# A two-block fp32 kernel whose queue orders are planned from TensorE's due times

## The chip, the core and the metric

The kernel runs on one core of a Trainium2 chip. A core has TensorE (PE: matmuls, with weight loads written PEld), VectorE (DVE), ScalarE (ACT), GpSimd (POOL) and SyncE (SP, which here only issues DMAs); POOL issues some DMAs too. Each engine works through its own queue strictly in order: an instruction that waits for another engine or for a DMA holds up everything behind it on its engine. PE's clock is granted by a throttle, and the profile tells the granted share. The metric is the device time of one execution in microseconds (us), and the median of several runs is compared.

## The reference, cut to what matters

Two transformer-like blocks follow each other on 512 tokens of width 2048, all in fp32. The first block puts 16 meta tokens ahead (528 rows) and has two mixers, A (grouped attention with axial rotary positions, 8 query heads, 2 key/value heads) and B (difference of two softmaxes, 8 heads). The second has stick-breaking attention (8 heads) and a gated linear recurrence (LRU, 8 blocks of channels).

```python
# first block
hn = rmsnorm(h, pre_norm_g)
qa, ka, va, ga, qb, kb, vb, gb = split(hn @ w_in)
ya = gqa_axial_mixer(qa, ka, va, ...) * silu(ga)       # softmax(q k^T) v per head
yb = diff_attn_mixer(qb, kb, vb, ...) * silu(gb)       # (softmax(s1) - lam*softmax(s2)) v, rmsnorm per head
h = h + rmsnorm(concat([ya, yb]) @ w_out, post_norm_g)
# second block
q, k, v, g_sb, x_lru, g_lru = split(rmsnorm_2(h) @ w_in_2)
y_sb  = stick_breaking_attention(rmsnorm_2(q), rmsnorm_2(k), v) * silu(g_sb)
y_lru = rg_lru(causal_depthwise_conv(x_lru)) * silu(g_lru)
out = h[meta removed] + concat([y_sb, y_lru]) @ w_out_2
```

## The kernel before

**Exact products from halves.** Every fp32 operand of a matmul is split into a high and a low half of type fp32r. The helper `split` (lines 167 to 169) casts on ACT (L168) and subtracts on DVE (L169). Each product is then three passes on PE (`PASSES`, line 396): high x high, high x low, low x high. So each tile of weights costs a DMA, an ACT cast and a DVE subtraction before PE can use it: `wraw` holds weights as loaded, `wsp` the halves. All matmuls are issued in `mm` (L201) and all transposes in `tr` (L204), so the tile names tell them apart in a profile: `pj` is a projection, `pss` scores or a transposed block, `ptt` the transposed probabilities, `pmt` the product of probabilities and values, `bank` the scores of the second block.

**Stages.** Keys, values and queries of A are projected first (to about 176 us of the span). Then follow 20 pairs of 128-column weight blocks (8 pairs for the two gates, 12 for q, k and v of B), each done by `seven` (line 431): a two-by-two scheme with seven products instead of eight on 12 of the 16 K tiles, the rest (`rest`) in the plain way. Its weight operands are sums of raw weight blocks, which accumulating DMAs form: `sum_up` (L356) issues them on POOL's queue, `load_raw` (L352) the plain loads on SP's, and `produce` (line 358) splits each operand and starts the next load into the slot that comes free. `side_x` (line 631) prepares the sums of activations for it (tiles `x23`, `x1s`). While `seven` runs for the gates (176 to about 370 us) attention of A goes on beside it, and after that attention of B. Then come the first output projection (O1), the second block's projections (XL, GL, GS, v, qk; weights through `load_next`, L320), its recurrence and attention beside these, and the second output projection (O2).

**A head of B.** `b_scores` (line 887) copies the new q and k into operand tiles, and then makes eight score tiles of 128 x 528: four matmuls into the only `pss` buffer, a DVE instruction that adds the bias and finds the minimum (L921), an ACT exponential (L924), and per pair two reciprocals, an ACT scaling (L936) and a DVE combination (L937). `b_sums` (line 943) calls `pv_steps` (line 696), which transposes the probabilities (`ptt`), splits them (`pt`, and `ptail`, L717 to L719, for the last 16 keys), multiplies with the values, normalises each head (L967 to L975) and sends it to DRAM (`yd`, L976). `fetch_y` (L618) reads it back and splits it into `big`, from which O1 reads. The projection of the next head may overwrite q and k when `b_scores` has copied them (key `qkused`).

**Who sets the order on PE.** Each piece of work is a Python generator. `run` (line 228) keeps a clock, to which each matmul adds an estimate of its time, and calls the first generator whose keys are all due: sides first, `main_work` last. A step that has handed work to another engine writes into `ready`, through `post(key, ns)` (line 210), when PE may go on with what depends on it: the clock plus `ns` times `pace[0]` plus 300 ns. From the first gate pair to the last value pair of B `pace[0]` is 1.35, else 1. Successive matmuls are tied by order-only edges (`_queue`, line 192), so PE's order is just the order in which the generators issued.

**Who sets the order elsewhere.** For ACT, DVE, POOL and SP there are no such edges, but for a few `issue_after` blocks that put activations behind a table load or another activation. Their queues come from the tile framework's own scheduler, which fills them by its own cost estimates.

Of the kernel before, what the change touches and what calls it, by code (L numbers as in the profile page):

```python
# [2 lines left out]

# [104 lines left out]
    return [(("KA", i), h) for h in range(2) for i in range(2)] + [(u, h) for u in seq for h in range(2)]  # L108


@with_exitstack
def hybrid_two_block_kernel(ctx: ExitStack, tc: tile.TileContext, wp, wq, wc, xT, xtok, par, lvec, cst, rg, pg, lruw, out):
    nc = tc.nc
    ctx.enter_context(nc.allow_low_precision("float32r halves of exact float32 splits"))
    act, dve, pool = nc.scalar, nc.vector, nc.gpsimd

    sb = ctx.enter_context(tc.tile_pool(name="sb", bufs=1))
    psj = ctx.enter_context(tc.tile_pool(name="psj", bufs=4, space=bass.MemoryType.PSUM))
# [1 line left out]
    dram = ctx.enter_context(tc.tile_pool(name="dram", bufs=1, space=bass.MemoryType.DRAM))  # L120

    def T(shape, tag, dt=F32, bufs=1):
        return sb.tile(shape, dt, tag=tag, name=tag, bufs=bufs)

    def small(n):
        return T([P, 16], "sm", F32, 16)[:, :n]

    def pjt():
        return psj.tile([P, 512], F32, tag="pj", name="pj")

    def evac2(dst, ps):

# [4 lines left out]
    pss_pool = [pss_stack.enter_context(tc.tile_pool(name="pss", bufs=1, space=bass.MemoryType.PSUM))]  # L137

    def pst():
        return pss_pool[0].tile([P, 2, 512], F32, tag="pss", name="pss")  # L140

    def pst_banks():

        return pss_pool[0].tile([P, 512], F32, tag="bank", name="bank", bufs=2)

    def ptt():
        return ps1.tile([P, 4, P], F32, tag="ptt", name="ptt")

    def pmt():
        return ps1.tile([P, 512], F32, tag="pmt", name="pmt")  # L150

    def et(n=L):
        return T([P, L], "e", F32, 6)[:, :n]
# [51 lines left out]

    HOP = 300.0

    pace = [1.0]

    def post(key, ns=0.0):  # L210
        ready[key] = state["clock"] + (ns * pace[0] + HOP if ns else 0.0)

    def hold(key):
        ready[key] = math.inf
# [10 lines left out]
    def when(*keys):  # L225
        return keys
# [27 lines left out]
    class Later:  # L254


        def __init__(self, make):
            self.make, self.tile = make, None
# [6 lines left out]
        def __getitem__(self, index):  # L265
            return self.whole()[index]

    turn = [None]

    def next_turn(shapes):  # L270

        if turn[0]:
            turn[0].close()
        turn[0] = ExitStack()
        pool_ = turn[0].enter_context(tc.tile_pool(name="turn", bufs=1))
        return [pool_.tile(sh, dt, tag=f"turn{i}", name=name) for i, (name, sh, dt) in enumerate(shapes)]

    early = Later(lambda: next_turn([("early", [P, KT * NTOK], F32)])[0])
    XO = 2 * KS * L
# [349 lines left out]
    gins = [0]  # L629

    def side_x():
        yield when(("kr", 0), ("kr", 1))

        def fetch(j):
            x = et(), et()
            for t, kt in zip(x, (j, KS + j)):
                nc.sync.dma_start(t, xT[kt])
# [138 lines left out]
    def side_kv(g):  # L776
        if g == 0:
            kt_[0] = T([P, 2, 2, L], "kk", F32R)
        yield when(("kv", 1), "rnat", "pss")
        kb, t1, u = (early[:, (3 * g + i) * 640 : (3 * g + i + 1) * 640] for i in range(3))  # L780
        dve.memset(kb[:, 512:640], 0.0)
        tp = flat(pst())
        for j in range(5):
            n = P if j < 4 else NM
            tr(tp[:n, j * P : (j + 1) * P], kvraw[g][:, tile_cols(j)], ident)
        dve.tensor_tensor(blocks(kb)[:, :4], blocks(tp[:, :512]),
                          rnat[:, 0:4].unsqueeze(2).broadcast_to([P, 4, P]), ALU.mult)
# [99 lines left out]
    def b_scores(h, e):  # L887
# [23 lines left out]
        def scores(qt, m, l):  # L911
# [4 lines left out]
            for c in range(2):  # L916
# [3 lines left out]
            b0 = 384 - qt * P  # L920
            dve.tensor_tensor_reduce(out=halves(x), in0=s[:, :, :HL], in1=halves(bias[:, b0 : b0 + L]),  # L921
                                     scale=1.0, scalar=3e38, op0=ALU.add, op1=ALU.min, accum_out=nm)
# [20 lines left out]
    def b_sums(h, e, vt):  # L943
# [19 lines left out]
        ssp = pmt()  # L963
        mm(ssp, ones_r, sh, True, False)
        mm(ssp, ones_r, sl, False, True)
        with tc.issue_after(lnload[0]):
# [75 lines left out]
    def side_lru(b):  # L1042
# [31 lines left out]
            pss_stack.close()  # L1074
            pss_pool[0] = ctx.enter_context(tc.tile_pool(name="psb", bufs=2, space=bass.MemoryType.PSUM))
        if b % 4 == 3:
            with tc.issue_after(ins):
# [15 lines left out]
    def sb_scores(h, e, vt):  # L1093
# [24 lines left out]
        for hf in range(2):  # L1118
            yield when(("qkt", h), "pss", "calm", 2)
            take_e(2)  # L1120
            for q2 in range(2):
# [3 lines left out]
                for pi, (a, b) in enumerate(PASSES):  # L1125
# [5 lines left out]
                with tc.issue_after(lnload[1]):  # L1131
# [43 lines left out]
    def main_work():  # L1175
# [88 lines left out]
        with tc.issue_after(last_tanh[0]):  # L1264
            lnload[0] = act.preload_act_table_set("natural_log_exp_and_others").ins

        ysplit = set()
# [135 lines left out]
        for h in range(8):  # L1403
# [4 lines left out]
        with tc.issue_after(ins):  # L1408
            lnload[1] = act.preload_act_table_set("natural_log_exp_and_others").ins

        def sb_v(c):
# [10 lines left out]
        def sb_qk(c):  # L1422
# [21 lines left out]
            yield from tm([("qk", c, kg) for kg in kgs], 0, evac, kgs, range(NT), *extra)  # L1444
            for t in range(NT):
                sq = et(512)
                with tc.issue_after(last[0]):
# [156 lines left out]
```

## Time and profile before

| | |
|---|---|
| median of 3 runs | 1773.55 us (1773.48 to 1774.43) |
| the profiled execution's own time | 1770.61 us |
| its span, first to last instruction | 1768.8 us |
| busy: PE / DVE / ACT / POOL | 1700.2 / 1110.1 / 902.2 / 151.6 us |
| matmuls, weight loads | 10288 each |
| mean granted clock of PE | 0.986 |

Durations and waits come from the profiled execution. A line of a view by stretches has the busy time of each engine within a stretch of the span and the granted clock there. A line of the order of time has start, duration, engine, line and operation, the tiles written and read, and in square brackets the engine's idle time before it and who ended that. "A <- B: t, n, m" says that A waited t us for B in n waits, m the longest. An "L" number is a line of the kernel, and a line of a helper stands for all that call it.

### The profile page before, as it was taken

To read this page: it belongs to the slowest core of one execution; us is meant where nothing else is said; L and a number is where in the kernel's file an instruction comes from. 1 tells how busy PE (TensorE), PEld (TensorE's weight loads), DVE (VectorE), ACT (ScalarE), POOL (GpSimd) and SP (SyncE) were. 2 spreads that over 40 slices of the span, in tenths; PEclk is the share of its full clock that TensorE was granted. 3 is DMA by queue.
4 is the path that set the end of the run, shared out by engine and by line. 5 is a ranking of instruction groups with operands and counts; after the bars stand their busy time and mean duration, and the time that the engine had idled before them with its cause. 6 is when DMAs were issued, how large, how long until landed. Compare 5 with 4: busy or idle time off the path is not lost.

```text
span 1768.8 us, 26488 instructions
## 1 busy us (share of the span) xinstructions
PE 1700.2 (96%) x10288; PEld 1509.4 (85%) x10288; DVE 1110.1 (63%) x1861; ACT 902.2 (51%) x1493; POOL 151.6 (9%) x165
## 2 busy tenths in 40 slices
PE   8999989998999898899699999999999999999999
PEld 7789889998999888888588999888888888888887
DVE  5774687776688777786358767843323575486433
ACT  6454555566466656566345547742222564475311
POOL 0111121211121121101000000100000000000000
PEclk9999999999999899999899999999999999999999
DMA  8436766765566454553267764233322222432223
GB/s 299 158 128 142 189 143 166 168 170 128 126 151 146 104 138 99 135 185 90 72 214 262 227 187 149 92 96 96 96 94 90 83 79 73 142 120 84 84 85 130
DMA packets 85550, 239.58 MB, mean 135 GB/s; under 512 B 9632, under 2 KB 15392, under 8 KB 83744
## 3 DMA queue, kind: packets, MB, share of 16 engines
q1 hardware_dynamic: 73904, 206.43, 36.6%
q0 software_dynamic: 11520, 31.46, 11.2%
q8 instruction: 80, 1.31, 0.3%
q14 instruction: 46, 0.38, 0.1%
HBM read 220.03 MB, written 17.83 MB: 134 GB/s over the span
## 4 chain that ended last, share of the span: by engine, by line
PE 56%; DVE 1%; DMA 1%; ACT 0%; issue 0%; DVEq 0%; ACTq 0%; SPq 0%
PE pj L201 51%; PE pmt L201 2%; PE pss L201 1%; PE bank L201 1%; PE ptt L204 1%; PE pmt L204 0%; PE pss L204 0%; DMA wraw<-in_wp 0%; DMA wraw<-in_wq 0%; DVE wsp L169 0%; DMA yd<-xmisc 0%; DMA e<-yd 0%; DVE pt L169 0%; ACT wsp L168 0%; DVE ptail L719 0%
## 5 line engine op out<-in xcount | busy, mean ns | idle before, releaser
L201 PE MATMUL pj<-wsp,big 128*128 128x512 f32 x3072 | 738.0, 397 | 10.2 <-ACT big L168 10.2
L201 PEld LDWEIGHTS pj<-wsp,big 128*128 128x128 f32 x3072 | 571.8, 189 | 138.4 <-ACT big L168 10.6
L201 PE MATMUL pj<-big,wsp 128*128 128x264 f32 (+3 forms) x4320 | 636.4, 304 | 15.1 <-ACT big L546 5.5
L169 DVE TENSOR_TENSOR wsp<-wraw,wsp 128x1024 fp32r<-128x1024 f32 (+3 forms) x399 | 426.1, 1070 | 336.8 <-ACT wsp L168 329.7
L201 PEld LDWEIGHTS pj<-big,wsp 128*128 128x128 f32 x4320 | 581.3, 189 | 53.2 <-ACT xmisc L457 5.9
L168 ACT CAST wsp<-wraw 128x1024 fp32r<-128x1024 f32 (+3 forms) x399 | 366.9, 922 | 459.3 <-PE pj L201 349.4
L356 POOL DMA_DIRECT2D wraw<-in_wq x80 | 70.0, 888 | 467.1 <-DVE wsp L169 294.3
L201 PE MATMUL pj<-x,wsp 128*128 128x264 f32 x720 | 98.7, 288 | 0.5 <-DVE wsp L169 0.5
L201 PEld LDWEIGHTS pj<-x,wsp 128*128 128x128 f32 x720 | 93.2, 192 | 0.8 <-DVE wsp L169 0.7
L201 PE MATMUL pmt<-pt,vv 128*128 128x256 f32 (+1 forms) x528 | 75.9, 296 | 16.8 <-DVE ptail L719 14.1
L201 PEld LDWEIGHTS pmt<-pt,vv 128*128 128x128 f32 x528 | 72.4, 203 | 21.0 <-DVE ptail L719 14.7
L201 PE MATMUL pss<-kk,qq 128*128 128x264 f32 x448 | 76.4, 300 | 7.4 <-DVE sm L921 7.1
L169 DVE TENSOR_TENSOR pt<-ptt,pt 128x512 fp32r<-128x512 f32 (+2 forms) x96 | 59.3, 618 | 27.1 <-ACT pt L168 26.7
L201 PEld LDWEIGHTS pss<-kk,qq 128*128 128x128 f32 x448 | 65.2, 198 | 11.9 <-DVE sm L921 7.6
L924 ACT ACTIVATE e<-e,sm 128x528 f32<-128x528 f32 x64 | 47.1, 736 | 38.5 <-DVE sm L921 38.0
L168 ACT CAST pt<-ptt 128x512 fp32r<-128x512 f32 (+2 forms) x96 | 50.3, 524 | 28.5 <-PE ptt L204 28.0
L204 PE MATMUL ptt<-ident,e 128*128 128x128 f32 x336 | 53.9, 278 | 8.6 <-DVE e L937 6.2
L921 DVE CUSTOM_DVE_ANT_0 e<-pss,ar 128x528 f32<-128x528 f32 x64 | 44.9, 702 | 26.0 <-PE pss L201 25.6
L1129 POOL TENSOR_SCALAR_AFFINE_SELECT e<-e 128x128 f32<-128x128 f32 x32 | 12.8, 401 | 478.7 <-ACT e L1128 470.8
L204 PEld LDWEIGHTS ptt<-ident,e 128*128 128x128 f32 x336 | 40.6, 142 | 12.8 <-DVE e L937 6.7
L201 PE MATMUL pj<-x1s,wsp 128*128 128x264 f32 x360 | 48.6, 285 | 2.4 <-DVE e L1241 2.4
L201 PEld LDWEIGHTS pj<-x1s,wsp 128*128 128x128 f32 x360 | 45.8, 188 | 2.9 <-DVE e L1241 2.6
(254 smaller groups left out, 1391.3 us busy)
## 6 DMA issues: line engine op xcount, KB each, us to landing
wraw<-in_wp SPq DMA_DIRECT2D x215, 512.0 KB, 3.6
wraw<-in_wq SPq DMA_DIRECT2D x80, 384.0 KB, 4.0
wraw<-in_wq POOLq DMA_DIRECT2D x80, 384.0 KB, 5.0
wraw<-in_wc SPq DMA_DIRECT2D x40, 256.0 KB, 3.2
e<-in_xT SPq DMA_DIRECT2D x28, 264.0 KB, 3.8
early<-in_xtok SPq DMA_DIRECT2D x4, 1024.0 KB, 6.9
gated<-e SPq DMA_DIRECT2D x16, 256.0 KB, 3.6
e<-yd SPq DMA_DIRECT2D x16, 256.0 KB, 3.7
```

Of the source, the lines that this page charges most:

```text
L168: act.copy(hi, src)
L169: dve.tensor_tensor(lo, src, f(hi), ALU.subtract)
L201: _queue(nc.tensor.matmul(out, lhsT, rhs, start=start, stop=stop).ins, cost)
L204: _queue(nc.tensor.transpose(out, in_, identity).ins, 110.0)
L356: pool.dma_start(pair_raw[(p, r)], wq[p, q], accum_op=ALU.add)
L921: dve.tensor_tensor_reduce(out=halves(x), in0=s[:, :, :HL], in1=halves(bias[:, b0 : b0 + L]), scale=1.0, scalar=3e38, op0=ALU.add, op1=ALU ...
L924: act.activation(x, x, AF.Exp, scale=-1.0, bias=nm, accum_out=l[:, m : m + 1])
L1129: pool.affine_select(z[:, t * P : w], z[:, t * P : w], [[-1, P]], ALU.is_gt, -1e30, base=0, channel_multiplier=1)
```

## The change

A class `Plan` is added. Its object is called for every instruction that the program creates. It notes the engine, a duration (`cost`: until its result is there; `busy`: how long it holds its engine), and what it depends on, found from the regions read and written, and from the order in which buffers of one tag are reused (`own`). When the whole program exists, `order()` gives every instruction a due time: for a matmul, the sum of the durations of the matmuls before it; for any other, the earliest due time of what needs it, less its own duration and 40 ns. Then it simulates all engines and, whenever one of ACT, DVE, POOL or SP is free, takes from its ready instructions the one that is due first. Up to 60 us of PE's due time a DMA is held until 8 us before it is due. An activation that needs another table is ranked 4 us later. The order found is then fixed by order-only edges along each of those four engines. PE's edges stay as they are.

Four smaller edits change what `run` is told: `pace` is gone (factor 1 throughout), the score buffer of B is posted after 2600 ns and not 3800, and `side_x` waits for a new key, `kf`, posted when a key head's transposes have been issued, where it waited for `kr`, the estimated end of that head's rotary step. `issue_after` is wrapped so that the plan sees these edges.

```diff
+class Plan:
+    HOP = 40.0
+    LEAD, SETTLED = 8000.0, 60000.0
...
+    def _costs(self, ins, e, op, n, width):
+        if e == "PE":
+            t = max(107.0, 4.4 + 0.4464 * n) if "float32r" in width else max(28.0, 0.8 * n)
+            return t + 60.0, t
+        if e == "DVE":
+            t = 150.0 + (2.08 if op == "TensorTensorScan" else 1.05) * n
+            return t, t - 70.0
+        if e == "Activation":
+            t = 200.0 + 0.85 * n + (190.0 if len(ins.outs) > 1 else 0.0)
+            return t, t - 80.0
+        t = {"TensorTensor": 400.0 + 2.6 * n, "TensorScalarPtr": 200.0 + 3.0 * n}.get(op, 400.0)
+        return t, t
...
+            cost, busy = (1300.0 + nb / 260.0, 60.0) if e == "SP" else (3300.0 + nb / 220.0, 870.0)
...
+    def order(self):
...
+        for i in range(N):
+            if self.engine[i] == "PE":
+                due[i] = t
+                t += self.busy[i]
+        for i in range(N - 1, -1, -1):
+            if self.engine[i] != "PE":
+                due[i] = min([due[j] for j in succs[i]] + [t]) - self.cost[i] - self.HOP
+                due[i] = min([due[i]] + [due[j] for j in heirs[i]])
...
+        def wanted(i):
+            now = due[pe[min(pe_next, len(pe) - 1)]]
+            return not self.nbytes[i] or now > self.SETTLED or due[i] - self.LEAD <= now
...
+                def rank(i):
+                    other = e == "Activation" and self.ins[i] and self.switch(i, table[0])
+                    return due[i] + (4000.0 if other else 0.0)
+
+                i = min((i for i in ready[e] if at[i] <= s and (eager or wanted(i))), key=rank)
...
+            if self.nbytes[i]:
+                lat = 1300.0 if e == "SP" else 2400.0
+                pipe = max(clock[e] + lat / 2, pipe) + self.nbytes[i] * (1.0 if e == "SP" else 1.2) / 260.0
+                end = pipe + lat / 2
...
+    plan = Plan()
+    nc.push_inst_callback(plan)
...
-    pace = [1.0]
     def post(key, ns=0.0):
-        ready[key] = state["clock"] + (ns * pace[0] + HOP if ns else 0.0)
+        ready[key] = state["clock"] + (ns + HOP if ns else 0.0)
...
     def side_x():
-        yield when(("kr", 0), ("kr", 1))
+        yield when(("kf", 0), ("kf", 1))
...
             tr(tb[:, j * P : j * P + n], t1[:n, j * P : (j + 1) * P], ident[:n, :n])
+        post(("kf", g))
...
-            post("pss", 3800)
+            post("pss", 2600.0)
             act.activation(x, x, AF.Exp, scale=-1.0, bias=nm, accum_out=l[:, m : m + 1])
...
-        pace[0] = 1.35
...
-        pace[0] = 1.0
...
     run(main_work(), sides)
+    nc.pop_inst_callback()
+    for e, nodes in plan.order().items():
+        if e != "PE":
+            for a, b in zip(nodes, nodes[1:]):
+                tc.add_manual_dep(plan.ins[b], plan.ins[a].name, order_only, reason="order planned")
```

More of the change, by code (lines that the diff above doesn't have):

```diff
@@ L1 @@
 import math
-from contextlib import ExitStack
+from contextlib import ExitStack, contextmanager
 import concourse.bass as bass
@@ L115, in hybrid_two_block_kernel, with issue_after @@
     act, dve, pool = nc.scalar, nc.vector, nc.gpsimd
+    plan = Plan()
+    nc.push_inst_callback(plan)
+    @contextmanager
+    def issue_after(ins):
+        plan.behind = ins
+        with tc.issue_after(ins):
+            yield
+        plan.behind = None
     sb = ctx.enter_context(tc.tile_pool(name="sb", bufs=1))
@@ L122, in T @@
     def T(shape, tag, dt=F32, bufs=1):
-        return sb.tile(shape, dt, tag=tag, name=tag, bufs=bufs)
+        return plan.own(sb.tile(shape, dt, tag=tag, name=tag, bufs=bufs), tag, bufs)
     def small(n):
@@ L128, in pjt @@
     def pjt():
-        return psj.tile([P, 512], F32, tag="pj", name="pj")
+        return plan.own(psj.tile([P, 512], F32, tag="pj", name="pj"), "pj", 4)
     def evac2(dst, ps):
@@ L139, in pst @@
     def pst():
-        return pss_pool[0].tile([P, 2, 512], F32, tag="pss", name="pss")
+        return plan.own(pss_pool[0].tile([P, 2, 512], F32, tag="pss", name="pss"), "pss", 1)
     def pst_banks():
-        return pss_pool[0].tile([P, 512], F32, tag="bank", name="bank", bufs=2)
+        t = pss_pool[0].tile([P, 512], F32, tag="bank", name="bank", bufs=2)
+        return plan.own(t, "bank", 2, plan.history["pss"][-1:])
     def ptt():
-        return ps1.tile([P, 4, P], F32, tag="ptt", name="ptt")
+        return plan.own(ps1.tile([P, 4, P], F32, tag="ptt", name="ptt"), "ptt", 1)
     def pmt():
-        return ps1.tile([P, 512], F32, tag="pmt", name="pmt")
+        return plan.own(ps1.tile([P, 512], F32, tag="pmt", name="pmt"), "pmt", 1)
     def et(n=L):
@@ L266, in __getitem__ @@
             return self.whole()[index]
-    turn = [None]
+    turn, turn_names = [None], []
     def next_turn(shapes):
@@ L275, in next_turn @@
         pool_ = turn[0].enter_context(tc.tile_pool(name="turn", bufs=1))
-        return [pool_.tile(sh, dt, tag=f"turn{i}", name=name) for i, (name, sh, dt) in enumerate(shapes)]
+        before, made = list(turn_names), []
+        turn_names.clear()
+        for i, (name, sh, dt) in enumerate(shapes):
+            t = plan.own(pool_.tile(sh, dt, tag=f"turn{i}", name=name), name, 1, before)
+            turn_names.append(t.name)
+            made.append(t)
+        return made
     early = Later(lambda: next_turn([("early", [P, KT * NTOK], F32)])[0])
@@ L965, in b_sums @@
         mm(ssp, ones_r, sl, False, True)
-        with tc.issue_after(lnload[0]):
+        with issue_after(lnload[0]):
             act.activation(orr, ssp, AF.Ln, scale=1.0 / P, bias=eps_tile)
@@ L1076, in side_lru @@
         if b % 4 == 3:
-            with tc.issue_after(ins):
+            with issue_after(ins):
                 for i in range(b - 3, b + 1):
@@ L1130, in sb_scores @@
                                    base=0, channel_multiplier=1)
-                with tc.issue_after(lnload[1]):
+                with issue_after(lnload[1]):
                     act.activation(l, z, AF.Abs)
@@ L1263, in main_work @@
                 yield from gates(name, i)
-        with tc.issue_after(last_tanh[0]):
+        with issue_after(last_tanh[0]):
             lnload[0] = act.preload_act_table_set("natural_log_exp_and_others").ins
@@ L1407, in main_work @@
             ins = silu2(ps, rb2, ybuf[:, h, :])
-        with tc.issue_after(ins):
+        with issue_after(ins):
             lnload[1] = act.preload_act_table_set("natural_log_exp_and_others").ins
@@ L1446, in sb_qk @@
                 sq = et(512)
-                with tc.issue_after(last[0]):
+                with issue_after(last[0]):
                     act.activation(sq, raw[:, t, :], AF.Square)
```

184 lines of the change are left out of this document (added).

## The prediction

> **What bounds the kernel now.** I read the page's span and busy times first, then busy times by stage, then the stretches at half clock, then who ends TensorE's waits.
>
> ```profile
> span 1768.8 us, 26488 instructions
> PE 1700.2 (96%) x10288; PEld 1509.4 (85%) x10288; DVE 1110.1 (63%) x1861; ACT 902.2 (51%) x1493; POOL 151.6 (9%) x165
> ```
>
> TensorE (PE) is the bound: idle for 1768.8 - 1700.2 = 68.6 us. By stage (columns: stretch and length; PE, weight load, DVE, ACT, POOL busy; granted clock; DMA share; GB/s):
>
> ```profile
> 0.00:44.00 44.00, 35.88 (x260) 34.00 (x261) 23.40 (x44) 28.44 (x42) 0.83 (x7) 1.00 0.84 298
> 44.00:176.00 132.00, 130.46 (x726) 112.19 (x725) 84.68 (x173) 62.11 (x95) 17.07 (x18) 1.00 0.49 143
> 176.00:430.00 254.00, 242.22 (x2010) 238.93 (x2008) 182.92 (x331) 141.81 (x256) 40.38 (x43) 1.00 0.69 164
> 430.00:572.00 142.00, 134.81 (x1088) 133.02 (x1087) 106.30 (x203) 86.31 (x160) 25.34 (x25) 0.98 0.60 136
> 572.00:772.00 200.00, 178.35 (x1339) 172.25 (x1339) 153.13 (x296) 122.95 (x235) 34.87 (x28) 0.93 0.53 126
> 772.00:836.00 64.00, 64.00 (x337) 54.09 (x336) 45.55 (x89) 42.85 (x82) 6.03 (x3) 1.00 0.41 131
> 836.00:880.00 44.00, 29.81 (x135) 23.71 (x134) 17.84 (x28) 16.15 (x32) 1.77 (x1) 0.84 0.23 72
> 880.00:1768.80 888.80, 884.71 (x4409) 741.25 (x4407) 496.30 (x701) 401.54 (x593) 25.36 (x40) 1.00 0.39 124
> ```
>
> Length less PE's busy time: 8.12 us idle at the start, 1.54, then 11.78 (gates and the A heads), 7.19 and 21.65 (the B heads), none, 14.19 (behind the last head), and 4.09, nearly all behind the last matmul. The second half holds nothing to win.
>
> Idle time is not all of it. Of the six stretches at half clock, the first three, the last and the sum of all:
>
> ```profile
> 437.40:444.20 6.80, 5.30 (x23) 4.87 (x24) 2.60 (x7) 2.85 (x7) 0.00 (x0) 0.50 0.01 2
> 580.70:590.90 10.20, 7.51 (x33) 7.06 (x34) 6.36 (x16) 6.74 (x15) 0.15 (x1) 0.50 0.24 69
> 645.60:649.00 3.40, 3.40 (x18) 3.40 (x18) 1.35 (x4) 1.73 (x6) 0.87 (x1) 0.50 0.25 99
> ...
> 864.00:877.60 13.60, 6.08 (x14) 4.53 (x15) 2.50 (x4) 1.34 (x3) 0.00 (x0) 0.50 0.31 109
> sum 47.60, PE 33.76 PEld 30.86 DVE 20.50 ACT 21.60 POOL 2.00; mean PE 5.63 PEld 5.14 DVE 3.42 ACT 3.60 POOL 0.33
> ```
>
> PE worked 33.76 us at half speed, so 16.9 us are lost: 5.30/2 = 2.65 before 572, 6.08/2 = 3.04 after 864, and (33.76 - 11.38)/2 = 11.2 between 572 and 772.
>
> Why it waits, in the order of time near 740 us:
>
> ```profile
> 736.87 0.65 PE L201 MATMUL pss<-kk,qq 128*128 128x264 f32 x4
> ...
> 739.05 1.35 ACT L168 CAST wsp<-wraw 128x768 fp32r<-128x768 f32 x2 [3.98 <-DMA wraw<-in_wq]
> 739.91 0.96 DVE L169 TENSOR_TENSOR wsp<-wraw,wsp 128x768 fp32r<-128x768 f32 x1 [3.54 <-ACT wsp L168]
> 740.79 0.70 DVE L921 CUSTOM_DVE_ANT_0 e<-pss,ar 128x528 f32<-128x528 f32 x1
> ...
> 741.55 0.75 PE L201 MATMUL pss<-kk,qq 128*128 128x264 f32 x4 [1.31 <-DVE sm L921]
> ```
>
> The scores were in PSUM at 736.87 + 0.65 = 737.52, but their reduction (L921) stood on DVE behind a weight split, that behind a cast on ACT, and that behind an accumulating DMA. DVE stood idle for 3.54 us with ready work behind its head. That is queue order, and this change rewrites queue order. The sum of such blocking from 176 to 772 us (us, times, longest):
>
> ```profile
> ACT wsp L168 <- DMA wraw<-in_wq: 50.1, 20, 4.1
> ```
>
> The other kind is PE's own order, at 574 to 586 us:
>
> ```profile
> 574.90 0.75 PE L201 MATMUL pss<-kk,qq 128*128 128x264 f32 x4 [0.44 <-DVE sm L921]
> 575.49 0.60 PE L204 MATMUL ptt<-ident,e 128*128 128x128 f32 x4
> 576.47 0.75 PE L201 MATMUL pss<-kk,qq 128*128 128x264 f32 x4 [0.37 <-DVE sm L921]
> 578.02 0.75 PE L201 MATMUL pss<-kk,qq 128*128 128x264 f32 x4 [0.81 <-DVE sm L921]
> 582.13 1.11 PE L204 MATMUL ptt<-ident,e 128*128 128x128 f32 x4 [3.36 <-DVE e L937]
> ```
>
> No projection (pj) stands between the steps of attention: the projection of the next head waits until this head's queries are copied, and the generator had spread the scores too thinly before. A score can follow the last one in 578.02 - 576.47 = 1.55 us; the old plan books 3800 x 1.35 + 300 = 5430 ns.
>
> **The change part by part.** It removes no instruction and adds none. It adds edges that carry order alone along ACT, DVE, POOL and SP, and changes three inputs to PE's order.
>
> *PE's order.* A head of B has 8 scores: 8 x 5.43 = 43.4 us in the old clock, 8 x (2.6 + 0.3) = 23.2 in the new. One head goes with one and a half weight pairs. Two rows show the limits:
>
> ```profile
> 484.00:572.00 88.00, 86.32 (x712) 85.59 (x712) 73.48 (x138) 59.02 (x110) 19.02 (x17) 1.00 0.64 144
> 572.00:674.00 102.00, 91.24 (x700) 88.84 (x700) 77.84 (x151) 62.34 (x121) 19.19 (x16) 0.93 0.53 120
> ```
>
> 572 to 674 is one period of two heads and three pairs. PE's work in it at full clock is 91.24 less half of what ran in the dips at 580.7 and 645.6 (7.51 + 3.40), 85.8 us, or 42.9 a head. So scores at 43.4 decided the old plan, and at 23.2 no longer do: the jams thin out.
>
> *The queues' order.* DVE has 77.84 us to do in that period. With no stall PE needs 85.8, and DVE would be 91% busy. The row before shows PE hardly waiting (1.68 of 88 us) with DVE at 73.48/88 = 83.5%. If 83.5% is all that an in-order DVE can give, a period takes 77.84/0.835 = 93.2 us. Bounds 85.8 and 93.2 against 102; I take the middle, 89.5, since the planner sorts by need but DVE still waits on ACT. From 572 to 772 are 200/102 = 1.96 periods: 1.96 x 12.5 = **24.5 us** (17.3 to 31.8). From 430 to 572 7.19 + 2.65 = 9.8 are lost; half, **5 us** (0 to 9.8). From 176 to 430 the waits are short and of the same kind; half of 11.78, **6 us** (0 to 11.8).
>
> *Behind the last head.* Scores after 763 us, and the end of the chain:
>
> ```profile
> L201 PE MATMUL pss<-kk,qq x64: 278/283/291, 763.3 to 843.6; 128*128 128x264 f32 x64
> ```
>
> ```profile
> 870.85 0.62 ACT L168 CAST big<-e 128x512 fp32r<-128x512 f32 x1 [10.13 <-DMA e<-yd]
> ...
> 871.52 1.95 PE L201 MATMUL pj<-wsp,big 128*128 128x512 f32 x3 [10.16 <-ACT big L168]
> ```
>
> 64 matmuls are 16 scores: when B's projections end, two whole heads of scores are left, and the output projection runs out of other work before the last head's y has been through DRAM (yd). If the scores keep up, one head is left: about (843.6 - 763.3)/2 = 40 us less of chain against a loss of 14.19 + 3.04 = 17.2. I take **13 us** (0 to 17.2), as what stays of the jams also delays this chain.
>
> *Moved at no cost.* The loads of xT of side_x now wait for the keys' transposes (kf for kr):
>
> ```profile
> L637 SPq DMA_DIRECT2D e<-in_xT x12: 327/382/497, 68.9 to 101.0; - x12
> ```
>
> Their casts and differences feed the first pair at 176 us, so 75 us of QA and VA matmuls, in the stage that idles 1.54 us, lie over them. If these loads came later than the cover, each us would be one of PE's. All SP loads are reordered with them, and POOL's accumulating loads stand in one order with the bias and normalising multiplies. At the start (8.12 us idle, DMA share 0.84) loads are held until 8 us before need; I take 0 (-3 to +3). In the second half DVE is 496.30/888.80 = 56% busy; 0 (0 to +10).
>
> *Added waits.* The edges have no semaphore, but each fixes who stands behind a head that is late. The planner prices SP's loads of 384 KB at 1300 + 393216/260 = 2812 ns; the page says 4.0 us, and of POOL's 5.0, where the planner has 5.1:
>
> ```profile
> wraw<-in_wq SPq DMA_DIRECT2D x80, 384.0 KB, 4.0
> wraw<-in_wq POOLq DMA_DIRECT2D x80, 384.0 KB, 5.0
> ```
>
> Behind a cast placed 1.2 us too soon stand ACT's exponentials (L924), the splits of pt and the copy of p1s (L457), and behind its DVE half L921.
>
> **Sum.** 24.5 + 5 + 6 + 13 = 48.5: 1768.8 - 48.5 = 1720.3 us of span. The profiled execution took 1770.61 us and the median of the runs is 1773.55, 4.75 above the span: **1725 us**.
>
> One rule bears on the clock. The dip at 437.4 follows waits of which this is the longest (430 to 772 us):
>
> ```profile
> PE ptt L204 <- DVE pt L169: 2.4, 1, 2.4
> ```
>
> The Trainium skill ("TensorE: Matmul & The Clock Gate", Part 1) says that the clock halves after an idle window of about 3.4 us; this trace disagrees, since several waits of up to 2.4 us sufficed. By the rule, short waits that are left would cost no clock; by the trace, a third of the 16.9 us might stay, 5.6 us more than my sum, which leaves no dip.
>
> A rule speaks against the planner's prices too. Here DVE ran under POOL:
>
> ```profile
> 255.61 1.20 DVE L169 TENSOR_TENSOR wsp<-wraw,wsp 128x512 fp32r<-128x512 f32 x1
> ```
>
> The planner prices that split at 150 + 1.05 x 512 = 688 ns. The Trainium skill ("SBUF — State Buffer", Summary: rules for kernel authors) says that a DVE operation with two SBUF inputs and a GpSimd one that reads SBUF block each other fully. The trace agrees here by 0.5 us; at 32 POOL operations in these stages that would be 16 us of unplanned DVE time, of which the 77.84 already hold what collides now.
>
> **The rivals.**
>
> *Everything comes back* (0.15): 11.78 + 9.8 + 32.8 + 17.2 = 71.7 of span, so 1702. For it: the waits have ready work behind them. Against: DVE at 91%.
>
> *DVE is the ceiling* (0.25): 83.5%, so 17.3 in the last stage of B, 2 before it, nothing in A, and 8 behind the last head, as scores lag again: 27, so 1746. For it: no row above shows PE busy with a busier DVE. Against: its idle time behind late casts.
>
> *The order is much the same* (0.06): the edges write down what the queues already did and PE's new order only moves the jams: 1773.
>
> *Slower: late loads at the head of ACT* (0.10). Place: the casts of wraw, 176 to 772 us. Price: 80 SP loads of 384 KB at 1.2 us each, 96 us of ACT standing still where 50.1 stand now. PE idles 11.78 + 7.19 + 21.65 = 40.6 there, 0.8 us per us of blocking. It decides from the point where over half of the 96 is met at the head; at all of it (96 - 50) x 0.8 = 37 us are lost, so about 1810. Against: ACT is 351.07/596 = 59% busy, so a cast seldom stands first at its landing.
>
> **How the numbers follow.** The forecast has 0.44: span gains of 35 to 62 us, 1711 to 1738. Two tenths are to lie outside the range: the slower case and no change above, little below. Low is the full recovery, 1702; high is 1766, a gain of 8 us, between the ceiling case and no change. Under 0.2% is what a measurement of this kernel can't tell from none: faster 0.44 + 0.15 + 0.25 = 0.84, same 0.06, slower 0.10.
>
> **What would show it.** PE idle of the stretch that answers to 176 to 772 at 15 to 25 us for 40.6, and one or no dip of the clock there for five. L921 starting within about 0.3 us of its matmuls' end. ACT's waits for wraw under 50.1 us. Eight scores, not 16, behind the last pair, and no wait of 10 us before the last O1 matmuls. DVE near 87% in B's stage. Wrong, if DVE's share stays under 80% while PE still waits, if the wait behind the last head stays, or if the second half shows PE idle before its end.

## The result, and the profile after

The changed kernel takes 1711.11 us (median of 4 runs, 1709.6 to 1713.94) against 1773.99 us for the kernel before: a ratio of 0.9644, with a 95% interval of 0.9627 to 0.9661. The profiled execution took 1711.61 us, its span is 1709.8. All lines of the code have moved by about 250: `mm` is now L450, `tr` L453, the split L417 and L418, B's score reduction L1175 (it was L921), the copy of p1s L710 (L457).

The page of the kernel after, its span and busy times:

```profile
span 1709.8 us, 26464 instructions
PE 1682.0 (98%) x10288; PEld 1497.2 (88%) x10288; DVE 1107.2 (65%) x1861; ACT 900.4 (53%) x1493; POOL 148.8 (9%) x165
```

The same matmuls, and 27.8 us of idle time on PE where 68.6 stood. To compare equal pieces of work, the span is cut at three matmuls: the first that reads a prepared sum of activations (tile `x`, in the first weight pair), the first of O1, and the first of XL in the second block. In the kernel before the first pair thus runs from about 158 us, not from 176 as the stages above have it. The stretches of the kernel before (length; PE, weight load, DVE, ACT, POOL busy; clock; DMA):

```profile
0.00:160.50 160.50, 150.84 (x852) 130.69 (x853) 99.60 (x203) 85.20 (x128) 15.27 (x22) 1.00 0.57 185
160.50:764.80 604.30, 564.11 (x4528) 554.26 (x4527) 443.92 (x832) 350.58 (x649) 103.23 (x99) 0.97 0.61 144
764.80:987.70 222.90, 208.29 (x989) 171.04 (x989) 141.67 (x221) 118.00 (x194) 7.79 (x4) 0.97 0.52 167
987.70:1768.80 781.10, 777.01 (x3925) 653.45 (x3923) 424.94 (x608) 348.39 (x523) 25.36 (x40) 1.00 0.35 110
```

And of the kernel after:

```profile
0.00:163.40 163.40, 152.29 (x852) 132.67 (x853) 100.02 (x203) 84.78 (x128) 16.44 (x22) 0.99 0.55 182
163.40:729.40 566.00, 557.00 (x4609) 551.48 (x4608) 454.11 (x868) 362.05 (x682) 105.91 (x101) 1.00 0.65 154
729.40:928.80 199.40, 195.81 (x906) 159.71 (x907) 127.27 (x185) 103.54 (x161) 3.15 (x2) 1.00 0.55 186
928.80:1709.80 781.00, 776.91 (x3925) 653.38 (x3923) 425.80 (x608) 349.98 (x523) 23.32 (x40) 1.00 0.35 110
```

The start lost 2.9 us, the pairs won 38.3, O1 won 23.5, and the second block is the same to 0.1 us. About 80 matmuls of attention, which ran beside O1, now run among the pairs (x4528 to x4609). PE's idle time among the pairs went from 604.30 - 564.11 = 40.2 us to 9.0, and the clock there from 0.97 to 1.00. What is left of PE's waits among the pairs (us, times, longest):

```profile
PE pj L450 <- ACT xmisc L710: 2.4, 2, 1.3
PE pj L450 <- DVE wsp L418: 2.1, 5, 0.9
PE pmt L450 <- DVE ptail L972: 2.0, 2, 1.6
PE pss L450 <- DVE vtail L946: 1.9, 2, 1.0
PE pmt L453 <- DVE ptail L972: 0.2, 1, 0.2
```

The jams of scores are gone, and behind the last pair only one head is left, 8 scores instead of 16:

```profile
L1175 DVE CUSTOM_DVE_ANT_0 e<-pss,ar x8: 694/698/708, 741.6 to 768.1; 128x528 f32<-128x528 f32 x8
```

One dip of the clock (3.4 us at half of full clock) stands inside the span. Order of time, and the stretch at half clock behind it:

```profile
61.31 0.94 PE L450 MATMUL pss<-e,ones 128*128 128x128 f32 x6 [2.28 <-DVE e L852]
```

```profile
62.90:66.30 3.40, 3.40 (x9) 2.62 (x10) 1.74 (x3) 0.58 (x2) 0.00 (x0) 0.51 0.00 0
```

This one is new. DVE computes the norm's reciprocal root just before, a chain of small operations. Three DVE rows in order of time, the middle one after a wait for ACT:

```profile
55.20 0.16 DVE L427 TENSOR_TENSOR sm<-sm 128x5 f32<-128x5 f32 x1
58.51 1.22 DVE L418 TENSOR_TENSOR wsp<-wraw,wsp 128x1024 fp32r<-128x1024 f32 x1 [3.15 <-ACT wsp L417]
59.65 0.16 DVE L428 SCALAR_TENSOR_TENSOR sm<-sm 128x5 f32<-128x5 f32 x1
```

A weight split that waits 3.15 us for ACT now stands between two links of the chain, and the norm waits with it.

The length of the wait alone does not decide about the dip. The same wait of 2.28 to 2.29 us stands at the same place in four of the kernels below (queues alone, edges on ACT and DVE, SP loads + 1.2 us, more DVE work), and half clock follows in the first of these only. In each profile the clock changes on a grid of 3.41 us. Here is the stretch of this grid before the dip, and then, for the kernel with SP loads + 1.2 us, the wait and the two stretches over which it falls:

```profile
59.49:62.90 3.41, 1.59 (x11) 1.45 (x12) 3.27 (x21) 0.08 (x1) 0.00 (x0) 1.00 0.56 159
```

```profile
59.40 1.48 PE L450 MATMUL pss<-e,ones 128*128 128x128 f32 x10 [2.29 <-DVE e L852]
```

```profile
55.15:58.57 3.42, 1.96 (x9) 1.26 (x7) 1.97 (x12) 1.46 (x4) 0.00 (x0) 1.00 0.31 123
58.57:61.98 3.41, 2.58 (x15) 2.25 (x16) 3.27 (x12) 0.66 (x2) 0.00 (x0) 1.00 0.48 159
```

PE was busy for 47% of the one stretch, and for 57% and 76% of the other two.

### The profile page after: what moved, and what is told of

Its sections match the earlier page's. It is cut to its first block, busy times and chain, and to the rows that moved or that the text cites. A ratio compares the mean times of both kernels' runs of the same rounds, so it can differ in the third digit from the quotient of the medians.

```text
span 1709.8 us, 26464 instructions
## 1 busy us (share of the span) xinstructions
PE 1682.0 (98%) x10288; PEld 1497.2 (88%) x10288; DVE 1107.2 (65%) x1861; ACT 900.4 (53%) x1493; POOL 148.8 (9%) x165
## 3 DMA queue, kind: packets, MB, share of 16 engines
q0 software_dynamic: 11520, 31.46, 11.5%
## 4 chain that ended last, share of the span: by engine, by line
PE 67%; DVE 4%; DMA 1%; ACT 1%; issue 1%; ACTq 0%; POOLq 0%; DVEq 0%; SPq 0%
PE pj L450 60%; PE pmt L450 2%; PE pss L450 2%; DMA wraw<-in_wq 1%; DVE wsp L418 1%; PE ptt L453 1%; PE bank L450 1%; PE pmt L453 1%; PE pss L453 1%; ACT wsp L417 1%; DVE e L1175 1%; DVE ar L1223 0%; DVE e L1191 0%; ACT e L1190 0%; DVE pt L418 0%
## 5 line engine op out<-in xcount | busy, mean ns | idle before, releaser
L450 PE MATMUL pj<-wsp,big 128*128 128x512 f32 x3072 | 734.5, 396 | 3.0 <-ACT wsp L417 1.0
L450 PEld LDWEIGHTS pj<-wsp,big 128*128 128x128 f32 x3072 | 571.7, 188 | 133.3 <-DVE big L418 1.6
L418 DVE TENSOR_TENSOR wsp<-wraw,wsp 128x1024 fp32r<-128x1024 f32 (+3 forms) x399 | 427.5, 1074 | 342.2 <-ACT wsp L417 336.2
L450 PE MATMUL pj<-big,wsp 128*128 128x264 f32 (+3 forms) x4320 | 635.3, 304 | 10.0 <-ACT wsp L417 7.2
L450 PEld LDWEIGHTS pj<-big,wsp 128*128 128x128 f32 x4320 | 582.5, 189 | 45.7 <-ACT wsp L417 7.5
L417 ACT CAST wsp<-wraw 128x1024 fp32r<-128x1024 f32 (+3 forms) x399 | 367.3, 923 | 444.5 <-PE pj L450 353.4
L450 PE MATMUL pj<-x,wsp 128*128 128x264 f32 x720 | 100.8, 286 | 1.9 <-DVE wsp L418 1.9
L450 PEld LDWEIGHTS pj<-x,wsp 128*128 128x128 f32 x720 | 92.5, 188 | 3.0 <-DVE wsp L418 2.7
L417 ACT CAST pt<-ptt 128x512 fp32r<-128x512 f32 (+2 forms) x96 | 50.7, 528 | 50.0 <-PE ptt L453 48.5
L418 DVE TENSOR_TENSOR pt<-ptt,pt 128x512 fp32r<-128x512 f32 (+2 forms) x96 | 59.5, 620 | 24.5 <-ACT pt L417 24.1
L450 PE MATMUL pss<-kk,qq 128*128 128x264 f32 x448 | 72.1, 289 | 2.8 <-DVE vtail L946 1.9
L450 PE MATMUL pmt<-pt,vv 128*128 128x256 f32 (+1 forms) x528 | 69.7, 280 | 2.1 <-DVE ptail L972 2.0
L450 PEld LDWEIGHTS pmt<-pt,vv 128*128 128x128 f32 x528 | 67.1, 188 | 4.5 <-issue 2.0
L450 PEld LDWEIGHTS pss<-kk,qq 128*128 128x128 f32 x448 | 61.4, 188 | 5.4 <-PE ptt L453 2.6
L453 PE MATMUL ptt<-ident,e 128*128 128x128 f32 x336 | 52.5, 273 | 0.0
L450 PE MATMUL pj<-x1s,wsp 128*128 128x264 f32 x360 | 50.1, 286 | 0.0
L1175 DVE CUSTOM_DVE_ANT_0 e<-pss,ar 128x528 f32<-128x528 f32 x64 | 44.8, 700 | 3.4 <-PE pss L450 3.3
L450 PEld LDWEIGHTS pj<-x1s,wsp 128*128 128x128 f32 x360 | 46.2, 188 | 0.2
L453 PEld LDWEIGHTS ptt<-ident,e 128*128 128x128 f32 x336 | 39.8, 140 | 2.6
```

The costliest lines, as they stand in the source:

```text
L417: act.copy(hi, src)
L418: dve.tensor_tensor(lo, src, f(hi), ALU.subtract)
L450: _queue(nc.tensor.matmul(out, lhsT, rhs, start=start, stop=stop).ins, cost)
L453: _queue(nc.tensor.transpose(out, in_, identity).ins, 110.0)
```

## The experiments

Theory: PE's new order takes the jams away and the planned queues take the blocking behind late splits away, and both are needed for the whole gain. Rivals: either part alone brings it. Each kernel was timed beside the kernel before on the same chip; the stretches are of one profiled execution each. The chips differ: the kernel before takes 1774 to 1778 us on them, so small differences are better read from the ratios than from the medians. "Start" is up to the first matmul that reads tile `x`.

| kernel | ratio to before (95%) | median us | start | pairs | O1 | second block to the last matmul |
|---|---|---|---|---|---|---|
| before | 1 | 1773.99 | 160.5 | 604.3 | 222.8 | 777.0 |
| after | 0.9644 (0.9627 to 0.9661) | 1711.11 | 163.5 | 566.0 | 199.4 | 776.9 |
| PE's order alone | 0.9755 (0.973 to 0.978) | 1733.33 | 159.8 | 589.4 | 200.9 | 776.9 |
| queues alone | 0.9873 (0.9843 to 0.9903) | 1753.31 | 161.7 | 583.7 | 224.5 | 776.9 |
| edges on ACT, DVE | 0.9699 (0.967 to 0.9728) | 1722.41 | 166.1 | 570.8 | 202.7 | 776.9 |
| edges on SP, POOL | 0.9739 (0.9713 to 0.9766) | 1730.74 | 157.0 | 593.7 | 197.2 | 777.0 |
| before, 2600 ns | 0.9846 (0.983 to 0.9861) | 1748.38 | 160.4 | 595.3 | 211.0 | 776.9 |
| before, factor 1 | 0.9854 (0.9837 to 0.987) | 1750.16 | 159.9 | 593.0 | 219.7 | 776.9 |
| program order | 0.9668 (0.9654 to 0.9682) | 1716.61 | 163.7 | 570.1 | 200.5 | 777.0 |
| flat durations | 0.988 (0.9864 to 0.9896) | 1753.55 | 175.5 | 579.2 | 204.4 | 787.9 |
| SP loads + 1.2 us | 0.9584 (0.9568 to 0.96) | 1703.59 | 159.3 | 561.1 | 199.8 | 776.9 |
| free start | 0.9597 (0.9572 to 0.9621) | 1704.73 | 157.3 | 564.4 | 199.2 | 776.9 |
| more DVE work | 0.9677 (0.966 to 0.9694) | 1719.88 | 162.1 | 570.1 | 202.9 | 776.9 |
| SP loads + free start | 0.9548 (0.9517 to 0.9578) | 1699.82 | 158.5 | 562.0 | 199.7 | 777.0 |

### PE's order alone

```diff
     for e, nodes in plan.order().items():
-        if e != "PE":
+        if False:
```

> The changed kernel without the order edges on ScalarE, VectorE, GpSimd and SyncE; PE's order is that of the changed kernel. Both-needed theory: PE's new order asks for results sooner, the queues still block behind late weight splits, so only a part of the 63 us comes: 1735 to 1765 us, PE idle between the first pair and O1 still 20 to 40 us. Rival PE-order-alone: within 10 us of the changed kernel, 1705 to 1721. Rival queues-alone: no gain or a loss, 1765 to 1800.

The ratio 0.9755 is 2.45% of the 3.56% that the whole change brings, about 43 of 63 us. The median lies 1.7 us under the range of the both-needed theory and 12 us above that of PE's order alone; PE's idle time, below, is in the range expected. So the theory priced PE's order too low, and neither rival holds. The stretch of the pairs of this kernel, and PE's first waits in it:

```profile
159.80:749.20 589.40, 565.60 (x4609) 558.34 (x4608) 455.40 (x868) 361.85 (x682) 107.12 (x101) 0.99 0.63 147
```

```profile
PE pj L450 <- ACT xmisc L710: 10.6, 6, 3.7
PE pss L450 <- DVE sm L1175: 3.9, 3, 2.5
PE pmt L450 <- DVE qq L418: 2.4, 2, 1.3
```

The pairs are 14.9 us shorter and O1 21.9, nearly the whole gain of O1. PE idles 589.40 - 565.60 = 23.8 us among the pairs. The waits for the last steps of attention (ptail), which led in the kernel before, are no longer the first:

```profile
PE pmt L201 <- DVE ptail L719: 11.1, 6, 3.2
```

What leads is the copy of p1s (L710), a short ACT instruction that stands too far back in its queue: in its two longest waits (3.7 and 3.6 us) behind the casts of the next head's q and k.

### The queues alone

```diff
+    pace = [1.0]
     def post(key, ns=0.0):
-        ready[key] = state["clock"] + (ns + HOP if ns else 0.0)
+        ready[key] = state["clock"] + (ns * pace[0] + HOP if ns else 0.0)
...
-            post("pss", 2600.0)
+            post("pss", 3800)
...
+        pace[0] = 1.35
...
+        pace[0] = 1.0
```

> The plan and its edges, but PE's order as before (factor 1.35, 3800 ns for the score buffer; the key kf stays). Both-needed theory: the head-of-line blocking goes, the jams of scores stay, 1735 to 1755 us, and the wait behind the last head (10 us before) stays. Rival queues-alone: 1705 to 1721. Rival PE-order-alone: 1760 to 1780.

1.27%, as the both-needed theory had it (the key `kf` stays in this kernel). Two stretches, pairs and O1, and a wait:

```profile
161.70:745.30 583.60, 558.35 (x4527) 550.72 (x4526) 443.06 (x832) 352.73 (x650) 102.62 (x99) 0.98 0.64 150
745.30:969.80 224.50, 209.72 (x986) 171.98 (x987) 142.03 (x220) 117.26 (x193) 7.89 (x4) 0.96 0.50 165
```

```profile
PE pj L450 <- ACT big L417: 9.1, 1, 9.1
```

The pairs gain 20.6 us and O1 nothing: two heads are still left when it begins, and the wait behind the last of them stays. The two parts add up, 2.45% + 1.27% = 3.72% against 3.56%, within the intervals, as they should if they remove different waits.

### Which queues

```diff
     for e, nodes in plan.order().items():
-        if e != "PE":
+        if e in ("Activation", "DVE"):
```

> The changed kernel with the edges on ScalarE and VectorE only; the DMA queues (SyncE, GpSimd) are as the framework orders them. If the order of the compute queues is what counts: 1708 to 1722 us. If the order in which loads are issued counts as much: 1730 to 1760, with ScalarE waiting for wraw well over the 36.6 us of the changed kernel.

```diff
-        if e != "PE":
+        if e in ("SP", "Pool"):
```

> The changed kernel with the edges on SyncE and GpSimd only. If the compute queues count: as the kernel with no edges at all, within 8 us of it. If the issue of loads counts: at least half of the gain that the edges bring over it.

The edges on ACT and DVE give the pairs 18.6 us over PE's order alone (589.4 to 570.8). Those on SP and POOL alone give the pairs nothing (593.7), and the kernel stays within 8 us of the one with no edges, as expected if the compute queues count; on top of the others they bring 4.8 there. At the time of 1722.41 us the first kernel missed its upper bound by 0.4 us: the order of loads is not nothing. But ACT's waits for wraw among its pairs are 38.6 us, hardly over the 36.6 of the changed kernel. At the start it is the other way round: ACT's and DVE's edges cost 6.3 us (159.8 to 166.1), SP's and POOL's gain 2.8.

### Which of PE's edits

```diff
-            post("pss", 3800)
+            post("pss", 2600.0)
```

> The kernel before with one number changed: B's score buffer posted after 2600 ns, not 3800 (the factor 1.35 stays, so 3810 ns in all for 5430). Theory that the booked rate of scores made the jams: 8 x 3.81 = 30.5 us a head is under PE's 42.9, so the jams and the wait behind the last head go, and most of the 44 us that PE's order brought come: 1733 to 1745 us. Rival, that the factor on all other steps did it: 1762 to 1774.

```diff
-        pace[0] = 1.35
```

> The kernel before with the factor 1.35 gone (the score buffer at 3800 + 300 = 4100 ns, 8 x 4.1 = 32.8 us a head, under 42.9). Theory of the booked rate of scores: also most of the gain, 1733 to 1750 us. If steps posted that early find the framework's queues too slow, waits of ptail, xmisc and of the queries grow in the gates' stage and eat part of it: 1750 to 1770.

Each alone brings 1.5%, and together, with the key `kf`, 2.45%. Both were expected to bring most of the gain by one theory, that the booked rate of scores had only to come under PE's 42.9 us a head. The first missed that range by 3.4 us, and its rival by more; the second lies 0.2 us above the theory's range, just inside its rival's. In the first kernel, with the booked rate at 30.5 us a head, and in the second, at 32.8:

```profile
PE pss L201 <- DVE sm L921: 17.1, 8, 5.7
```

```profile
PE pj L201 <- ACT big L168: 9.1, 1, 9.1
```

With 2600 ns alone PE asks for scores while the framework's DVE queue is late for them, up to 5.7 us. With the factor alone the wait behind the last head stays. So the booked rate is not the whole story: the factor on the other steps counts as well. That asking early makes the wait is not shown: PE's order alone books 2.9 us a score, less than either, on the framework's queues too, and waits only 3.9 us for them (shown above). Why 2600 ns alone does worse stays open.

### Due times or durations

```diff
-                    return due[i] + (4000.0 if other else 0.0)
+                    return i
```

> The changed kernel, where each engine takes of its ready instructions the one created first, not the one due first. If due times carry the gain of the edges: most of the 22 us over the kernel without edges is lost, 1725 to 1745 us. If any order simulated with traced durations does: 1708 to 1718.

```diff
-            t = 150.0 + (2.08 if op == "TensorTensorScan" else 1.05) * n
+            t = 700.0
...
-            t = 200.0 + 0.85 * n + (190.0 if len(ins.outs) > 1 else 0.0)
+            t = 700.0
```

> The changed kernel, where the plan books 700 ns for every VectorE and ScalarE instruction, whatever its size (traced: 0.15 to 1.9 us). If the traced durations matter: the plan runs out of step, 1722 to 1750 us. If the due order alone matters: 1708 to 1718.

This was the surprise. With the first ready instruction in program order instead of the one due first, 0.9668 stands against 0.9644: the due times carry at most about a quarter of what the edges bring (5.5 us of medians where edges bring 22), and the intervals of the two ratios overlap. In this kernel due times still hold back early DMAs, and the later rank of activations that need another table is gone too. With due times but flat durations the kernel falls to 0.988, slower than with no edges at all (0.9755) and 3.6 us over the range expected. The first three stretches of that kernel:

```profile
0.00:175.50 175.50, 155.26 (x852) 134.12 (x853) 99.33 (x203) 84.38 (x128) 16.90 (x22) 0.95 0.52 170
175.50:754.70 579.20, 562.85 (x4610) 555.75 (x4608) 453.04 (x867) 362.93 (x681) 106.47 (x101) 0.99 0.64 149
754.70:959.10 204.40, 198.12 (x907) 162.06 (x906) 128.15 (x186) 103.99 (x162) 3.62 (x2) 0.98 0.57 185
```

It loses everywhere: 12 us at the start, 13.2 among the pairs, 5 in O1, and 11 in the second block (787.9 for 776.9), where no other kernel lost any. A reading that fits: what makes the planned queue good is that the instruction at its head is ready when the queue gets there, and a queue planned with wrong durations stays wrong. Whether the short instructions booked too long or the long ones booked too short do it was not tested.

### Late loads

```diff
-            cost, busy = (1300.0 + nb / 260.0, 60.0) if e == "SP" else (3300.0 + nb / 220.0, 870.0)
+            cost, busy = (2500.0 + nb / 260.0, 60.0) if e == "SP" else (3300.0 + nb / 220.0, 870.0)
...
-                lat = 1300.0 if e == "SP" else 2400.0
+                lat = 2500.0 if e == "SP" else 2400.0
```

> The changed kernel, where the plan books SyncE's loads 1.2 us longer (2500 ns and the bytes; 4012 ns for 384 KB, traced 4.0). Rival of the prediction, that casts placed too early for late loads cost time: ScalarE's waits for wraw fall well under 36.6 us and the time to 1700 to 1708 us. If casts seldom stand first when their load lands: within 4 us of the changed kernel, 1707 to 1716.

The rival's mechanism is there. ACT's waits for these weights among the pairs, of the kernel after, of this one, and of PE's order alone:

```profile
ACT wsp L417 <- DMA wraw<-in_wq: 36.6, 15, 4.7
```

```profile
ACT wsp L417 <- DMA wraw<-in_wq: 23.9, 12, 3.9
```

```profile
ACT wsp L417 <- DMA wraw<-in_wq: 33.1, 20, 4.7
```

12.7 us less of waiting go with 4.9 us among the pairs and 4.2 at the start; 0.9584 against 0.9644. Of the 4.2, 1.7 are the dip, which this kernel lacks by the place of its wait on the clock's grid alone (see above): that part is luck. The third row says how little this sum tells by itself: without any edges ACT waits less for loads than in the kernel after, and PE idles 23.8 us there for 9.0. What counts is what stands behind the waiting cast.

### The start

```diff
     for e, nodes in plan.order().items():
+        if e in ("Activation", "DVE"):
+            nodes = [i for i in nodes if plan.start[i] > 100e3]
         if e != "PE":
```

> The changed kernel, where ScalarE and VectorE get their edges only from 100 us of the planned time on; SyncE and GpSimd keep theirs throughout. Theory that the planned order of ScalarE and VectorE costs some 6 us before the first pair (163.4 us with all edges, 157.0 with those of SyncE and GpSimd alone): 1702 to 1707 us. Rival, that what is gained ahead is lost behind, since the plan no longer fits: 1709 to 1716.

The start takes 157.3 us instead of 163.5, and nothing is lost behind it: the planned order of ACT and DVE cost 6 us at the start, as the pair of kernels above had said. The norm's scores come without a wait, and no dip follows:

```profile
56.84 1.37 PE L450 MATMUL pss<-e,ones 128*128 128x128 f32 x10
```

They begin 4.5 us sooner than in the changed kernel: 2.28 are the wait and 2.2 are won ahead of it; the dip's 1.7 us complete the 6.2.

### More work for DVE

```diff
+            if m == 0:
+                dve.tensor_tensor(x, bias[:, b0 : b0 + L], bias[:, b0 : b0 + L], ALU.add)
             dve.tensor_tensor_reduce(out=halves(x), in0=s[:, :, :HL], in1=halves(bias[:, b0 : b0 + L]),
```

> The changed kernel with one more VectorE addition (128 x 528, about 0.7 us) ahead of every other score of B, which the plan knows and which writes a tile that the score overwrites: 32 x 0.7 = 22 us more VectorE work from 431 to 768 us, where VectorE is about 87% busy and would come to 94%. If VectorE is the ceiling below 90%: 1725 to 1735 us. If it still has room: 1711 to 1717.

1719.88 us lies between the two ranges. From the first score of B to the last, the kernel after and this one:

```profile
431.70:768.00 336.30, 330.65 (x2602) 321.05 (x2601) 293.71 (x575) 235.95 (x458) 64.36 (x54) 1.00 0.61 149
```

```profile
428.30:772.60 344.30, 334.95 (x2601) 324.93 (x2600) 310.66 (x604) 237.21 (x458) 65.22 (x54) 0.99 0.61 145
```

DVE goes from 293.71/336.30 = 87.3% to 310.66/344.30 = 90.2% busy. It does 17.0 us more in a stretch that is 8.0 us longer. So 83.5% was no ceiling, nor is 87.3%, but the room above is not free either: nearly half of the added work shows in the time. The added instruction also takes its score's tile, one of six, early (the first at 396 us, its score at 428), and how much of the 8.0 us that costs was not tested.

### Both improvements

> The changed kernel with both: SyncE's loads booked 1.2 us longer, and the edges of ScalarE and VectorE only from 100 us of the planned time on. If the two gains are separate (pairs and start): 1697 to 1702 us. If the longer booking already holds the gain at the start (its first pair begins at 159.3 us, 157.3 with the free start): 1701 to 1705.

At 0.9548 it is the fastest kernel run, 4.5% under the kernel before and about 1% under the change. The time lies in the range for gains that add. But the runs behind it go from 1698.35 to 1703.1 us, the interval overlaps that of the longer booking alone, and in the profiled execution neither the start (158.5 us for the free start's 157.3) nor the pairs (562.0 for the longer booking's 561.1) is better than with the one edit. Whether the gains add in full stays open.

## Why the prediction was right, and where its sizes were off

*The sum.* 1725 us was forecast and 1711.11 measured, inside the range and at the far edge of the forecast's own band: 48.5 us of span were to come, and 59.0 came. The number is not owed to errors that cancel: the terms for the pairs and for the last head both came out larger than booked, and only the start went the other way, by 3 us.

*PE's order.* Right in kind: the scores no longer decide, the jams are gone, one head is left behind the last pair. But the working gave this step no price of its own. It put the gain into the queues' term, and that was the wrong weight: PE's order alone, three small edits (two booked numbers and a key), is two thirds of the whole. The total holds all the same, since the period of two heads from which it was worked out has both parts in it.

*The queues' order.* Here is the term that was mis-sized. The three terms for 176 to 772 us came to 35.5 us. Lost among the pairs before were 40.2 us of idle time and 13.9 at half clock (5.30/2 + 11.2), 54 in all; after, 9.0 of idle time and no dip, so 45 came back. The failing step is the choice of the middle between 85.8 and 93.2 us a period. From B's first score to the first score of its seventh head are three such periods, before and after:

```profile
438.70:763.30 324.60, 300.31 (x2349) 294.49 (x2348) 246.46 (x476) 195.90 (x369) 58.29 (x50) 0.95 0.55 128
```

```profile
431.70:686.80 255.10, 252.94 (x2085) 250.89 (x2084) 222.90 (x441) 178.03 (x346) 55.69 (x47) 1.00 0.63 143
```

One takes 108.2 us before and 85.0 after, the stall-free end: PE idles 2.2 of the 255.1 us, and DVE is 87.4% busy. The upper bound rested on DVE's 83.5% in a stretch where PE hardly waited, but that was what the work there asked of DVE and not what DVE can give, as the kernel with more DVE work shows.

*Behind the last head.* 13 us against 17.2 lost: the stretch of O1 now idles 199.40 - 195.81 = 3.6 us at full clock, where it idled 14.6 and lost 3.0 at half clock, so 14 came back. The rest of the 23.5 us is attention that moved among the pairs.

*At no cost.* The second block was right to 0.1 us. The start cost 2.9 us, at the edge of the bounds given, by a cause that was not named: the split put inside the norm's chain, with the wait of 2.28 us and the dip of 1.7 that came with it. With ACT and DVE free at the start both are gone.

*The evidence from the queues.* That a score stood behind a split and this behind a load was read rightly, and the edges do remove such waits (queues alone, 20.6 us among the pairs). Of the signs, the dips, DVE's 87% and the eight scores came as named, and PE's idle time among the pairs fell further, to 9.0 us for the 15 to 25 named. One sign failed: L921 was to start within about 0.3 us of its matmuls' end. The median from there to the reduction's start is 0.49 us before, 0.28 with the queues alone and 0.79 in the kernel after (64 scores each). In the full change the reductions do not come sooner; PE only waits for them no longer, 7.1 us among the pairs before and none after. And the sum of ACT's waits for wraw, offered as a sign, is none, as the third row on late loads shows.

*The rivals.* Everything comes back: in the main, 56 of the 71.7 us by idle time and half clock among pairs and O1 less the start (45 + 14 - 3). DVE as the ceiling: refuted at 83.5%. Order much the same: refuted, and the queues alone are worth 1.3%. Late loads: a cost of some 8 us by the medians and 11 by the ratios, not a loss; 12.7 us of ACT's waiting went with 4.9 among the pairs, 0.4 us per us, half of what the rival's price assumed.

*The clock.* The rows decide against the rule of the Trainium skill ("TensorE: Matmul & The Clock Gate", Part 1) as quoted, here again: half clock followed a wait of 2.28 us, and PE was busy for 1.59 of the 3.41 us before the dip. But no rule by the longest wait replaces it, as the same wait without a dip shows. The 5.6 us kept for such dips were not needed: one dip cost 3.40/2 = 1.7 us.

## What to carry to other kernels

In a queue that runs in order, ask of each wait what stands behind the waiting instruction, not how long it waits; if the queue is planned, the durations have to come from a trace, since here the due times mattered little, if at all, and flat durations were worse than no plan. Before planning queues, look at the bound engine's own order: here it was two thirds of the gain and three small edits in the code. A busy share seen in a quiet stretch is a demand and no limit; to learn the limit, add work.

## What the runs showed of the hardware

A DVE operation can last more than twice as long beside a POOL one. The square of orr (L969 before, L1223 after, 128 x 512) by min/median/max ns, before and after:

```profile
L969 DVE TENSOR_TENSOR ar<-ar x8: 691/693/1819, 525.7 to 860.8; 128x512 f32<-128x512 f32 x8
```

```profile
L1223 DVE TENSOR_TENSOR ar<-ar x8: 692/1585/2225, 493.2 to 793.5; 128x512 f32<-128x512 f32 x8
```

POOL's multiply by the same orr follows the same ACT instruction. Eight of these sixteen squares are slow, 1.45 to 2.23 us: three before, five after. In all eight POOL's multiply ran beside the square and had begun before it or at most 0.03 us after it. Of the eight others, at 0.69 us, three ran without it, and five began at least 0.04 us ahead of it. In all fourteen profiles no square without the multiply beside it took over 0.70 us (16 squares), and 51 of the 96 with it took 1.1 us or more. The plan books 688 ns for each. That this contention is the cause rests on these rows; no run took the multiply away. The eight squares take 11.5 us of DVE time after and 8.8 before, and none of PE's waits shown above is for them.

The granted clock goes by stretches of 3.41 us. Counted over the fourteen profiles, at full clock and from PE's first matmul on, half clock followed 48 of the 49 stretches in which PE was busy for under 45%, and none of the 6813 in which it was busy for over 65%. In between both occur.
